# One transformer layer with a mixture of experts on one core: the last tile's router logits from its raw sum, and two pairs gathered by TensorE

## The chip, the core and the metric

The kernel runs on one core of one Trainium2 chip. What is compared is the device time of one execution, in microseconds (us). Engines are TensorE (PE in the profile; PEld is its weight load), VectorE (DVE), ScalarE (ACT), GpSimd (POOL) and SyncE (SP, which here only issues transfers; SPq is its queue).

## What is computed

One layer with a post-norm residual path, on 512 tokens of 1024 numbers:

```
h  <- LN(alpha*h + W_out[concat(norm(A(h)), norm(B(h)))])
h  <- LN(alpha*h + HierMoE(h))
...
gl = t @ w_group + b_group;  pg = softmax(gl);  g_idx = top_k(gl, 1)
el = (t @ w_expert + b_expert)[the 8 experts of g_idx]
top_v, top_i = top_k(el, 2);  w = pg[g_idx] * softmax(top_v)
for e in range(32):
    hid = silu(t @ w_gate[e]) * (t @ w_up[e])
    y   = y + combine[:, e:e+1] * (hid @ w_down[e])
```

A is an attention over a window of 128 positions to either side (8 heads of 64), B a dense latent attention (8 heads). Four groups of eight experts: a token goes to one group and in it to two experts.

## The kernel before

The 512 tokens are four tiles of 128 (0, 1, a = 2, b = 3). Attention B runs first, then attention A, tile after tile; then come for each tile the output projection of A's heads, the residual sum z, its layer norm, the router logits and the routing. For tiles 0 to 2 most of this lies between the matmuls of later tiles of attention A; for tile b it comes after the last attention matmul. Up to there a scheduler sets the order on each engine from the code's dependences, in the part of the experts the code's own order holds (`manual_schedule`).

The names of the routing, in the order of one tile: `turn` transposes the normed tile by TensorE, `logits` multiplies it with `wr` (the 4 columns of the groups and 32 of the experts), `biased` adds the bias (lgt), `route` finds the group and the two experts in ten short VectorE steps, and ends with Mb, a 0/1 matrix of token by expert; `count` and `place` make from it (by matmuls with triangular ones) the place of each token in its expert's 64 slots (posm); `weights` makes the two routing weights (cmb); `select` writes the 0/1 matrix of token by slot (sel); `places_mm` multiplies sel and cmb, so that each slot gets its token's number and weight, and `places_end` splits these.

The experts are handled in 16 pairs: a pair's 64 + 64 slots are the 128 rows of one tile. `fetch` lets POOL gather the tokens' rows from HBM by an indirect DMA (xg), `columns` transposes them (p_x to xT), `gates` runs the gate and up matmuls (p_gu, L1081, 8 steps k of 128 rows for two experts side by side), `gated` forms hid, `down` the second matmul (p_y, L1101), and `scatter` lets POOL write the weighted rows back to HBM (moe_rows) by an indirect DMA. The weights lie in a ring of 6 expert slots; `load_next` issues those of pair p + 3 on SyncE's queue behind the gates of pair p, in order. The last two pairs (14 and 15, `NCOMB`) are not scattered: their rows are combined on TensorE by products with sT (pz). In the end the two sets of 512 rows in HBM are loaded (rows0, rows1), summed, added to pz (`total`), normed (`square`, `factor`, `scale`, `gain`, `bias`) and written out.

The router's weights are loaded ahead of attention A, behind w_out's rows and the norm's factors:

```python
wr = rl_.tile([P, NK, 36], F32, name="wr")
SY.dma_start(out=wr[:, :, 0:4], in_=A["w_group"][0].rearrange("(k p) g -> p k g", p=P))
SY.dma_start(out=wr[:, :, 4:36], in_=A["w_expert"][0].rearrange("(k p) g -> p k g", p=P))
```

The `wout` generator loads w_out's rows and splits them into woah (ScalarE) and woal (VectorE, L521).

## Time and profile before

| | |
|---|---|
| time, median of 3 (lowest to highest) | 617.35 us (616.49 to 619.59) |
| profiled execution: time, span | 618.7 us, 617.0 us |
| mean granted clock of TensorE | 0.939 |
| busy: TensorE, VectorE, ScalarE, POOL | 534.0, 328.7, 204.7, 132.3 us |
| bytes over DMA | 137.91 MB, 223 GB/s over the span |

The busy times are sums over stages with different limits, so they say little alone; which engine or queue ends last is read by stretch. The clock is a share of full speed, and TensorE's two levels are 1.2 and 2.4 GHz, 0.5 and 1.0.

### The profile page before, as it was taken

What the parts mean: (1) busy time and instruction counts of PE and PEld (TensorE: products, weight loads), DVE (VectorE), ACT (ScalarE), POOL (GpSimd) and SP (SyncE); (2) the same over time, 40 slices, a digit from 0 to 9 for tenths busy, and PEclk for the clock granted to TensorE, in tenths of its full rate; (3) what the DMA queues carried; (4) which work ended last, traced back from release to release, by engine and by line L of the source; (5) the groups of instructions that cost most, each with busy time, mean ns of one, the idle gap of its engine ahead of it and who ended that gap; (6) DMA issues with size and microseconds to landing.
All of it is one profiled execution on the core that took longest, in us unless ns stands there. A gap on an engine that the chain in (4) does not pass through costs nothing. (4 is left out here: it accounts for less than half of the span.)

```text
span 617.0 us, 8276 instructions
## 1 busy us (share of the span) xinstructions
PE 534.0 (87%) x2886; PEld 341.7 (55%) x2887; DVE 328.7 (53%) x870; ACT 204.7 (33%) x428; POOL 132.3 (21%) x161
## 2 busy tenths in 40 slices
PE   3799999999899999999974899999997798768950
PEld 2688998799677777777763433333352232313330
DVE  5954465665896667977887343232431121102177
ACT  3174442544674356655510221112111010211131
POOL 2601122211433232213110211211111101000265
PEclk9799999999999999999985799999998899969975
DMA  8803400321220008960437499999999999998263
GB/s 293 246 2 78 136 1 18 107 79 39 86 70 1 1 1 242 396 258 36 172 114 295 122 381 421 416 412 420 419 412 409 420 412 385 422 420 330 76 257 136
DMA packets 42044, 137.91 MB, mean 223 GB/s; under 512 B 12168, under 2 KB 15112, under 8 KB 32784
## 3 DMA queue, kind: packets, MB, share of 16 engines
q1 hardware_dynamic: 36240, 126.86, 53.9%
q0 software_dynamic: 4608, 8.40, 3.7%
q10 hardware_dynamic: 1152, 2.10, 0.9%
q8 instruction: 24, 0.39, 0.3%
q14 instruction: 20, 0.16, 0.1%
HBM read 133.13 MB, written 12.58 MB: 236 GB/s over the span
## 5 line engine op out<-in xcount | busy, mean ns | idle before, releaser
L1081 PE MATMUL p_gu<-w_gu,xT 128*64 128x512 f32 x512 | 129.4, 626 | 16.9 <-DMA w_gu<-in_w_gu 16.9
L1081 PEld LDWEIGHTS p_gu<-w_gu,xT 128*64 128x64 f32 x512 | 41.5, 144 | 99.2 <-issue 73.3
L1086 DVE TENSOR_TENSOR hid<-hid,p_gu 128x256 f32<-128x256 f32 x16 | 6.7, 421 | 116.2 <-ACT hid L1085 116.2
L1101 PE MATMUL p_y<-w_dn,hidT 128*64 128x512 f32 x256 | 59.3, 598 | 1.1 <-issue 0.6
L1085 ACT ACTIVATE hid<-p_gu 128x256 f32<-128x256 f32 x16 | 6.1, 384 | 162.8 <-PE p_gu L1081 162.6
L1113 DVE SCALAR_TENSOR_TENSOR xg<-p_y,wsl,xg 128x512 f32<-128x512 f32 x28 | 21.0, 751 | 40.3 <-PE p_y L1101 40.0
L931 POOL DMA_INDIRECT xg<-norm_rows,tok x16 | 16.7, 1046 | 113.8 <-issue 39.0
L1106 POOL DMA_INDIRECT moe_rows<-xg,idx x16 | 16.5, 1033 | 109.7 <-DVE xg L1113 93.9
L1101 PEld LDWEIGHTS p_y<-w_dn,hidT 128*64 128x64 f32 x256 | 18.2, 137 | 30.8 <-issue 28.3
L592 PE MATMUL ptr<-cst,pr 128*128 128x128 f32 x208 | 34.7, 280 | 0.0
L554 POOL TENSOR_SCALAR pr<-pr,rc 128x512 f32<-128x512 f32 x16 | 25.0, 1565 | 43.6 <-DVE rc L553 43.6
L594 ACT COPY pT<-ptr 128x512 f32<-128x512 f32 (+2 forms) x48 | 22.6, 478 | 27.4 <-PE ptr L592 25.1
L592 PEld LDWEIGHTS ptr<-cst,pr 128*128 128x128 f32 x208 | 24.6, 141 | 7.5 <-issue 4.3
L567 ACT ACTIVATE pr<-pmm,bnm 128x512 f32<-128x512 f32 x32 | 22.1, 690 | 16.6 <-DVE bnm L564 13.8
L216 PE MATMUL pmm<-wh,htl 128*128 128x512 f32 (+1 forms) x64 | 24.1, 376 | 0.0
L214 PE MATMUL pmm<-wh,hth 128*128 128x512 f32 (+1 forms) x64 | 24.1, 376 | 0.0
L564 DVE TENSOR_REDUCE bnm<-pmm 128x1 f32<-128x512 f32 x32 | 21.8, 686 | 4.0 <-PE pmm L216 3.8
L215 PE MATMUL pmm<-wl,hth 128*128 128x512 f32 (+1 forms) x64 | 23.8, 372 | 0.0
L615 PE MATMUL pac<-pT,vb 128*64 128x128 f32 x256 | 23.7, 282 | 0.0
L1066 PEld LDWEIGHTS p_x<-cst,xg 128*128 128x128 f32 x128 | 14.8, 146 | 14.2 <-issue 8.1
L1066 PE MATMUL p_x<-cst,xg 128*128 128x128 f32 x128 | 20.6, 289 | 2.0 <-DMA xg<-norm_rows,tok 2.0
L586 ACT ACTIVATE pr<-sm,anm 128x257 f32<-128x257 f32 (+1 forms) x32 | 18.2, 569 | 12.2 <-PE ptr L592 6.1
(305 smaller groups left out, 1182.5 us busy)
## 6 DMA issues: line engine op xcount, KB each, us to landing
w_gu<-in_w_gu SPq DMA_DIRECT2D x52, 1024.0 KB, 16.5
...
```

The source lines that it names most:

```text
L214: PE.matmul(ps, ah, bh, start=first, stop=False)
L215: PE.matmul(ps, ah, bl, start=False, stop=False)
L216: PE.matmul(ps, al, bh, start=False, stop=last)
L554: eng.tensor_scalar(pr[:, :n], pr[:, :n], rc, None, ALU.mult)
L564: V.tensor_reduce(nm, sp, AX.X, ALU.max, negate=True)
L567: exps.append(SC.activation(pr[:, :S], sp, AF.Exp, bias=nm, accum_out=den).ins)
L592: PE.transpose(pt[:, k * P:(k + 1) * P], pr[:, k * P:(k + 1) * P], ident)
L594: ev(pT[:, :n * P], pt[:, :n * P])
L615: PE.matmul(po[64 * j:64 * j + 64, h0 // 2 * P:h0 // 2 * P + P], vfn(k0 + k, h), pp[j][:, k * P:(k + 1) * P], start=(k == 0), stop=(k == n ...
L1066: PE.transpose(pt[:, k], pl["xg"][:, P * (4 * j2 + k):P * (4 * j2 + k) + P], ident)
L1081: PE.matmul(pg[64 * i:64 * i + 64], xT[:, j, 64 * i:64 * i + 64], ws[i][0][j], start=(j == 0), stop=(j == 7))
L1101: PE.matmul(py[64 * i:64 * i + 64, :], hT[:, j, 64 * i:64 * i + 64], ws[i][1][n][:, j], start=(j == 0), stop=(j == 1))
```

## The change

Three things change. First, the last tile's logits no longer wait for its layer norm: ahead of attention A, wr is multiplied by the norm's gain and offset (wg, wb; gb_T is a new input that holds both, turned), and the column sums of both products are formed by 16 matmuls with ones. The last tile's raw sum is turned and multiplied with wg, and mean and deviation come in afterwards on the 36 logits. Second, the first two pairs are not fetched for their columns: TensorE multiplies the normed tiles with the 0/1 matrices sel0 (`gather`, 32 matmuls of 128x256), which gives xT directly; their rows are still fetched, for the residual. The first two pairs' weights come after the rows' numbers, and pair 0's gates are parted in steps 0 to 4 and 5 to 7 with the weights' matmuls between. Third, pair 14 is scattered as the others are, only pair 15 is combined by products, and the order at the end is written anew.

```diff
         lg2, lb2 = lngb[:, 0], lngb[:, 1]
+        gbT = rl_.tile([P, 2, NK], F32, name="gbT")
+        SY.dma_start(out=gbT, in_=A["gb_T"])
         wr = rl_.tile([P, NK, 36], F32, name="wr")
...
+        onesf = trif
+        V.memset(onesf, 1.0)
+        wg = rp_.tile([P, NK, 36], F32, name="wg")
+        wb = scr.tile([P, 385], F32, name="sm", bufs=2)[:, :NK * 36].rearrange("p (a b) -> p a b", a=NK)
+        for i, w_ in enumerate((wg, wb)):
+            V.tensor_tensor(w_, wr, gbT[:, i].unsqueeze(2).to_broadcast([P, NK, 36]), ALU.mult)
+        pgb = psd("sums")
+        for k in range(NK):
+            for i, w_ in enumerate((wg, wb)):
+                PE.matmul(pgb[:, 36 * i:36 * i + 36], onesf, w_[:, k], start=(k == 0 and i == 0), stop=(k == NK - 1 and i == 1))
+        wsum = rl_.tile([P, 36], F32, name="wsum")
+        SC.copy(wsum, pgb[:, 0:36])
+        rbias2 = rl_.tile([P, 36], F32, name="rbias2")
+        V.tensor_tensor(rbias2, pgb[:, 36:72], rbias, ALU.add)
+        sel0 = [rl_.tile([P, 4 * CAP], F32R, name="sel00")]
...
             for k in range(4 * i, 4 * i + 4):
-                PE.matmul(d["pl"][:, 0:36], d["hT"][i][:, k % 4 * P:k % 4 * P + P], wr[:, k, :], start=(k == 0), stop=(k == NK - 1))
+                w = wg[:, k, :] if t == NT - 1 else wr[:, k, :]
+                PE.matmul(d["pl"][:, 0:36], d["hT"][i][:, k % 4 * P:k % 4 * P + P], w, start=(k == 0), stop=(k == NK - 1))
         def biased(t):
             d = tl[t]
-            d["lgt"] = rl_.tile([P, 36], F32, name="lgt", bufs=2)
+            d["lgt"] = rl_.tile([P, 36], F32, name="lgt", bufs=3)
+            if t == NT - 1:
+                V.scalar_tensor_tensor(d["lgt"], wsum, d["nm"], d["pl"][:, 0:36], ALU.mult, ALU.add)
+                V.scalar_tensor_tensor(d["lgt"], d["lgt"], d["rs"], rbias2, ALU.mult, ALU.add)
+                return
             V.tensor_tensor(d["lgt"], d["pl"][:, 0:36], rbias, ALU.add)
...
+            if t == 1:
+                return
             yield
             for _ in route(t):
                 pass
             yield
+            rows_of(t)
             weights(t)
+            yield
+            count(t)
+            place(t)
+            sel0_(t)
...
+        def gather(t, js):
+            for j in js:
+                q = j // 2
+                if gk[q] is None:
+                    gk[q] = ps.tile([P, 2, 4, CAP], F32, name="p_g", tag="pmm" if q < 2 else "pwo", bufs=2)
+                PE.matmul(gk[q][:, j % 2].rearrange("p a b -> p (a b)"), z[t][:, P * j:P * j + P],
+                          f32v(sel0[t]),
+                          start=(t == 0 and j % 2 == 0), stop=(t == NT - 1 and j % 2 == 1))
...
-        for u in range(2):
-            count(u)
-            place(u)
+        offset(a)
+        r1 = route(1)
+        for _ in range(5):
+            next(r1)
         V.tensor_tensor(ol, pv, f32v(oh), ALU.subtract)
+        for i in range(2):
+            scaled(a, i)
+        gather(0, range(4))
         p0 = wout_h(0)
         V.tensor_reduce(s1, sq.rearrange("p a b -> p b a"), AX.X, ALU.add)
-        norm_gain(a, 0)
         sp = psd("sum")
...
+        for _ in r1:
+            pass
+        gain(a, 0, V)
         rsqrt(rr, sp[:, 0:1], ALPHA ** 2 / 512, ALPHA ** 2 * RMS_EPS)
+        gain(a, 1, V)
+        shift(a, 0, PO)
         wout_l(0, p0)
-        norm_bias(a, 0)
-        norm_gain(a, 1)
-        norm_bias(a, 1)
+        shift(a, 1, PO)
         wout_l(1, p1_)
+        norm_tiles(b)
+        turn(b, 0)
         turn(a, 1)
         for i in range(2):
             keep(a, i)
+        count(1)
+        place(1)
+        logits(a, 0)
...
+        V.tensor_scalar(nm, mv[:, 0:1], -1.0, None, ALU.mult)
         logits(a, 1)
-        norm_gain(b, 0)
-        norm_bias(b, 0)
-        norm_gain(b, 1)
-        turn(b, 0)
-        norm_bias(b, 1)
         turn(b, 1)
-        for i in range(2):
-            keep(b, i)
         biased(a)
         ra, rb = route(a), route(b)
         for _ in ra:
             pass
         logits(b, 0)
         logits(b, 1)
+        offset(b)
+        for i in range(2):
+            scaled(b, i)
+        biased(b)
         count(a)
-        biased(b)
+        gather(1, range(4))
         for _ in range(4):
             next(rb)
         place(a)
+        sel0_(a)
+        gain(b, 0, PO)
+        shift(b, 0, PO)
+        gather(0, range(4, 8))
         for _ in rb:
             pass
         count(b)
-        weights(a)
-        for t in range(b):
-            sel0_(t)
-        pi0 = psd("places")
-        cms0 = [weights_of(p) for p in range(2)]
-        places_mm(pi0, sel0, cms0, range(b))
+        gather(1, range(4, 8))
+        gather(a, range(8))
+        gain(b, 1, V)
         place(b)
         sel0_(b)
-        weights(b)
-        places_mm(pi0, sel0, cms0, [b])
-        pls = places_end(pi0, 2)
-        for p in range(2):
+        shift(b, 1, PO)
+        for i in range(2):
+            keep(b, i)
+        gather(b, range(8))
...
+        gathered(0)
+        gathered(1)
+        pi0 = psd("places")
+        pairs = range(2)
+        for t in range(NT):
+            for u in pairs:
+                PE.matmul(pi0[:, 2 * u:2 * u + 2], sel0[t][:, P * u:P * u + P],
+                          cmb[t][:, 2 * u:2 * u + 2, 0], start=(t == 0 and u == 0), stop=(t == b and u == 1))
+        pls = places_rows(pi0, 2, 2, 1)
+        for p in pairs:
             fetch(p, pls[p])
-        overflow()
+        for t in (1, a, b):
+            weights(t)
...
+        def run_pair(p, xT, nx, meanwhile):
             pg = new_gates()
-            gates(pg, xT, ws[p], 0, 8)
+            if p == 0:
+                gates(pg, xT, ws[p], 0, 5)
+                pi = psd("places")
+                places_mm(pi, sel0, [weights_of(u) for u in range(2)], range(NT))
+                places_weights(pi, pls, 6, 3, 1)
+                gates(pg, xT, ws[p], 5, 8)
+            else:
+                gates(pg, xT, ws[p], 0, 8)
             load_next(p)
...
+            def meanwhile(i):
+                if p == 0:
+                    if i == 0:
+                        group(1)
+                        for u in (2, 3):
+                            fetch(u, plc[u])
+                    else:
+                        for u in range(2):
+                            residual(u)
+                        overflow()
+                    return
...
+        p = NP - 2
+        pg = new_gates()
+        gates(pg, xTs[0], ws[p], 0, 8)
+        leave_rows(gated(pg), ws[p], plc[p])
         for t in range(NT):
             for k, r in enumerate((rows0, rows1)):
                 SY.dma_start(out=r[t], in_=yd[S * k + t * P:S * k + (t + 1) * P, :])
...
+        p = NP - 1
+        pg = new_gates()
+        gates(pg, xTs[1], ws[p], 0, 8)
+        hT = gated(pg)
+        y2 = [ring(slots(p)[0], f"gu0{k}", [P, D], F32R, "y2") for k in range(2)]
+        y2 = halves(y2)
+        weighted(p, hT, y2)
+        for t in range(NT):
+            for n in range(2):
+                pz_part(t, n, sTs[0], y2)
...
         gbs = gb[:, 0], gb[:, 1]
+        for t in range(2):
+            for n in range(2):
+                rows_add(t, n, PO)
+        for n in range(2):
+            rows_add(2, n, V)
         total(0)
-        rows_add(1, 1, PO)
-        rows_add(2, 0, PO)
+        square(0)
+        for n in range(2):
+            rows_add(3, n, V)
         total(1)
-        rows_add(2, 1, V)
-        square(0)
         factor(0, True)
+        scale(0)
         square(1)
-        scale(0)
+        total(2)
         factor(1, True)
-        total(2)
         square(2)
-        rows_add(3, 0, PO)
-        rows_add(3, 1, PO)
+        total(3)
+        gain(0)
+        square(3)
         scale(1)
-        gain(0)
-        total(3)
-        square(3)
         bias(0)
+        gain_first(2)
+        factor(2, False)
+        scale_bias(2)
         gain(1)
+        bias(1)
         factor(3, False)
-        factor(2, False)
         gain_first(3)
         scale_bias(3)
-        gain_first(2)
-        bias(1)
-        scale_bias(2)
```

Three places of VectorE's order, before and after. The first is the start of attention A (L580 before and L579 after are its scores, by a custom instruction; woal is w_out's lower part; wg and sm, which holds wb, are the two products).

Before:

```order
L564 TENSOR_REDUCE bnm<-pmm 128x1
L580 ISA sm,anm<-pmm,mask,nsink 128x256
L580 ISA anm 128x1
L553 RECIPROCAL rc<-den 128x1
L594 COPY pT<-ptr 128x512
L554 TENSOR_SCALAR pr<-pr,rc 128x512
L580 ISA sm,anm<-pmm,mask,nsink 128x256
L580 ISA anm 128x1
L553 RECIPROCAL rc<-den 128x1
```

After:

```order
L520 SCALAR_TENSOR_TENSOR woal<-wf_2586,goa,woah 128x1024
L547 SCALAR_TENSOR_TENSOR z_67<-pwo,rr,z_67 128x512
L520 SCALAR_TENSOR_TENSOR woal<-wf_2587,goa,woah 128x1024
L547 SCALAR_TENSOR_TENSOR z_67<-pwo,rr,z_67 128x512
L520 SCALAR_TENSOR_TENSOR woal<-wf_2587,goa,woah 128x1024
L709 TENSOR_TENSOR wg<-wr,gbT 128x288
L709 TENSOR_TENSOR sm<-wr,gbT 128x288
L579 ISA sm,anm<-pmm,mask,nsink 128x256
L579 ISA anm 128x1
L552 RECIPROCAL rc<-den 128x1
```

The products and all of woal stand ahead of the first scores; before, the first woal stood behind eight score instructions.

The second is where the last attention rows are split (aol) and squared sums taken (asum), at the end of attention A. Before:

```order
L832 TENSOR_TENSOR w_3560<-w_3560,e_3552 128x1
L834 TENSOR_SCALAR wc<-M_3519,w_3560 128x32
L719 SCALAR_TENSOR_TENSOR posm_78<-psd,Mb_69 128x32
L984 TENSOR_TENSOR aol<-pac,aoh 128x512
L986 TENSOR_REDUCE asum<-asq 128x128
L737 SCALAR_TENSOR_TENSOR z_66<-z_66,ln_mv,lngb 128x512
L835 SCALAR_TENSOR_TENSOR wc<-M_3555,w_3560,wc 128x32
```

After:

```order
L798 TENSOR_TENSOR lgt<-psd,rbias 128x36
L805 TENSOR_REDUCE gm<-lgt 128x1
L809 SCALAR_TENSOR_TENSOR fc<-lgt,gm,cst 128x4
L812 TENSOR_REDUCE fm<-fc 128x1
L815 TENSOR_SCALAR G<-fc,fm 128x4
L818 TENSOR_TENSOR em<-lgt,G 128x32
L1060 TENSOR_TENSOR aol<-pac,aoh 128x512
L1065 TENSOR_REDUCE asum<-asq 128x128
L823 MAX mm<-em 128x8
L826 MAX_INDEX mi<-mm,em 128x8
```

Before, tile 1's whole route and its place (posm_78) stood ahead of the split; now the first five steps of the route stand there, fed by logits that come later on TensorE, and the others stand behind.

The third is the second residual sum of tile b (the z_67 with pwo). Before:

```order
L976 SCALAR_TENSOR_TENSOR z_67<-pwo,rr,z_67 128x512
L998 BN_STATS ln_st<-z_67 128x6
L741 SCALAR_TENSOR_TENSOR z_66<-z_66,ln_rs,lngb 128x512
L976 SCALAR_TENSOR_TENSOR z_67<-pwo,rr,z_67 128x512
L1005 BN_STATS ln_st<-z_67 128x6
L1009 BN_AGGR ln_mv<-ln_st 128x2
```

After:

```order
L1024 SCALAR_TENSOR_TENSOR z_67<-pwo,rr,z_67 128x512
L1079 BN_STATS ln_st<-z_67 128x6
L1298 MEMSET silu 128x1
L737 SCALAR_TENSOR_TENSOR posm_78<-psd,Mb_69 128x32
L1024 SCALAR_TENSOR_TENSOR z_67<-pwo,rr,z_67 128x512
L1091 BN_STATS ln_st<-z_67 128x6
L922 TENSOR_TENSOR sel<-posm_78,cst 128x256
L1097 BN_AGGR ln_mv<-ln_st 128x2
```

The place of tile 1 (posm_78), which waits for a count on TensorE, now stands between the two sums.

## Rows read from the trace of the kernel before

**Rows 1.** Busy us by stretch (columns: PE, PEld, DVE, ACT, POOL, clock, DMA share, GB/s).

```profile
235.25:247.15 11.90, 11.80 (x91) 9.16 (x90) 10.72 (x40) 9.25 (x24) 1.52 (x7) 1.00 1.00 312
247.15:300.00 52.85, 51.91 (x353) 39.84 (x351) 43.90 (x141) 31.71 (x88) 12.07 (x31) 1.00 0.58 227
307.33:344.68 37.35, 21.66 (x112) 18.67 (x113) 29.72 (x127) 5.46 (x16) 5.58 (x6) 0.67 0.47 177
344.68:356.00 11.32, 10.94 (x53) 4.76 (x54) 2.40 (x5) 4.36 (x5) 0.86 (x1) 0.87 0.58 170
356.00:565.00 209.00, 185.80 (x858) 71.64 (x854) 57.77 (x154) 30.07 (x44) 26.79 (x26) 0.96 1.01 412
```

**Rows 2.** Timeline of VectorE at the start of attention A.

```profile
235.25 0.48 DVE L580 CUSTOM_DVE_ANT_0 sm<-pmm,mask,nsink 128x256 f32<-128x256 f32 x1 [0.93 <-PE pmm L577]
245.94 1.28 DVE L521 SCALAR_TENSOR_TENSOR woal<-wf,goa,woah 128x1024 fp32r<-128x1024 f32 x1
```

**Rows 3.** Timeline of SyncE's queue there: the issue of wr's second load.

```profile
236.67 4.34 SPq L693 DMA_DIRECT2D wr<-in_w_expert  x1
```

**Rows 4.** DMA view: packets from 242 to 244 us, and from 246 to 248 us.

```profile
DMA packets 1317, 0.64 MB, mean 321 GB/s; under 512 B 1170, under 2 KB 1170, under 8 KB 1317
DMA packets 194, 0.73 MB, mean 365 GB/s; under 512 B 19, under 2 KB 19, under 8 KB 191
```

**Rows 5.** Timeline of TensorE, end of attention to pair 0, and pair 15.

```profile
300.70 0.39 PE L215 MATMUL pwo<-woal,aoh 128*128 128x512 f32 x1
303.26 0.60 PE L758 MATMUL psd<-cst,z 128*128 128x128 f32 x4
304.87 1.87 PE L769 MATMUL psd<-wr,h2T 128*128 128x36 f32 x16
306.67 0.66 PE L615 MATMUL pac<-pT,va 128*64 128x128 f32 x8
323.61 3.43 PE L769 MATMUL psd<-wr,h2T 128*128 128x36 f32 x16
342.78 1.97 PE L1066 MATMUL p_x<-cst,xg 128*128 128x128 f32 x8 [1.96 <-DMA xg<-norm_rows,tok]
344.68 8.48 PE L1081 MATMUL p_gu<-w_gu,xT 128*64 128x512 f32 x32
576.11 3.65 PE L1081 MATMUL p_gu<-w_gu,xT 128*64 128x512 f32 x16
```

**Rows 6.** Timeline of VectorE from the end of attention to the first weights.

```profile
306.78 0.20 DVE L774 TENSOR_TENSOR lgt<-psd,rbias 128x36 f32<-128x36 f32 x1 [1.14 <-PE psd L769]
310.15 0.68 DVE L984 TENSOR_TENSOR aol<-pac,aoh 128x512 fp32r<-128x512 f32 x1
317.79 0.75 DVE L976 SCALAR_TENSOR_TENSOR z<-pwo,rr,z 128x512 f32<-128x512 f32 x1 [0.69 <-PE pwo L972]
329.62 0.15 DVE L816 TENSOR_SCALAR gn<-gm 128x1 f32<-128x1 f32 x1
331.56 0.20 DVE L837 TENSOR_TENSOR cmb<-wc,cmb 128x32 fp32r<-128x32 f32 x1
```

**Rows 7.** Timelines of ScalarE and of SyncE's queue at pair 0.

```profile
345.95 1.28 ACT L1085 ACT_TABLE_LOAD   x1
348.04 7.22 SPq L649 DMA_DIRECT2D w_gu<-in_w_gu  x6
```

**Rows 8.** Timelines of POOL, SyncE's queue and VectorE in the tail.

```profile
571.46 0.98 POOL L1106 DMA_INDIRECT moe_rows<-xg,idx  x1 [8.45 <-DMA moe_rows<-xg,idx]
581.05 1.80 POOL L1274 MEMSET gb<- 128x2048 f32 x1 [3.53 <-DMA moe_rows<-xg,idx]
599.23 2.94 POOL L1286 TENSOR_TENSOR rows<-rows,rows 128x512 f32<-128x512 f32 x2
584.36 4.47 SPq L1279 DMA_DIRECT2D rows<-moe_rows  x8
591.43 0.69 DVE L1326 CUSTOM_DVE_ANT_0 rows<-pz,rows 128x512 f32<-128x512 f32 x1 [0.49 <-POOL rows L1286]
```

184 lines of the change are left out of this document (95 added, 89 removed).

## The prediction

> **What bounds the kernel now.** I read the busy time by stretch first [rows 1]. From attention A's first scores (235.25) to 300 TensorE is busy nearly all the time: 11.80 of 11.90 us, then 51.91 of 52.85. Its last attention matmul ends at 307.33 [rows 5]; I call that point T0. From T0 to the first expert matmul at 344.68 TensorE is busy 21.66 of 37.35 us at a mean clock of 0.67 of full, and VectorE 29.72: there the chain of small routing steps decides. From 356 to 565 the DMA share is 1.01 at 412 GB/s: the weights of the experts stream in, and nothing else counts. The stream is kept going by the ring of weight slots, and it starts when the first expert pair's matmuls free a slot: SyncE issues w_gu at 348.04, and that group of six issues lasts 7.22 us, since its later tiles wait for the last matmuls of the pair [rows 7]. So each us by which pair 0's matmuls end later is a us at the end, and so is each us in the tail behind the stream; what a change costs between 356 and 565 on the engines is hidden by the DMA.
>
> **Term 1: the sums of the weighted router weights, ahead of attention A.** The change forms wg and wb on VectorE and sums them with 16 matmuls of 36 columns. In the new order of VectorE both products, and all four woal instructions, stand ahead of the first score instruction of attention A; before, eight score instructions stood ahead of the first woal. The products wait for wr. Its second load is issued from 236.67 and takes the queue 4.34 us [rows 3]; it consists of small packets: 1170 of 1317 packets in 242 to 244 are under 512 B, and 19 of 194 in 246 to 248 [rows 4]. So wr is there at about 246. The first score instruction, at 235.25 before [rows 2], then starts at about 247.5: 12.2 us later. Queued behind it are all scores, so the softmax, the transposes and the value matmuls of attention A. TensorE does not lose all of it. Part of its 11.80 us in this stretch was the end of attention B (a tile's output projection and the last value products), which it does in any case, and two units of scores fit into the two PSUM buffers ahead of VectorE. I put the lost work at 5.5 us, a little under half of the 11.80, and 1.5 for refilling the pipeline; neither is measured, so the ends stay far apart below. The 16 matmuls cost 16 x 0.234 = 3.7 us (eight of the same width took 1.87 us [rows 5]). Against it, tile 1's logits (1.87) and four of its transposes (0.6) move behind T0, and the four 1.28-us woal instructions [rows 2] no longer lie between scores, which I price at 1.5 to 2. Sum: 5.5 + 1.5 + 3.7 - 2.5 - 1.7 = +6.5 us on T0. Bounds: 0, if everything in this stretch can be caught up later (TensorE was busy 51.91 of 52.85 us after it, which speaks against that), and +12, if the whole shift passes on.
>
> **Term 2: from T0 to pair 0's first matmul.** Before, 37.35 us. Now TensorE's queue holds behind its last attention matmul: four gathers, four transposes of tile 1, eight output-projection matmuls, eight logits. A gather is a 128x256 f32 matmul; Eight of the experts' matmuls of 512 columns (16 records) took 3.65 us, and two of them run side by side, each on half of the array [rows 5]. On the whole array that is four matmuls of 512 columns or eight of 256: a gather is worth about 0.43 to 0.46 us. An output-projection matmul takes 0.233 (eleven from 300.70 to 303.26), four transposes 0.60, eight logits 1.87 [rows 5]. Queue: 4 x 0.43 + 0.6 + 8 x 0.233 + 1.9 = 6.1 us. VectorE takes tile 1's logits then, and the split aol of the attention rows stands behind five steps of this routing; before, routing had begun at 306.78, and aol ran at 310.15, T0 + 2.8 [rows 6]. Now aol is at 6.1 + 1.4 = T0 + 7.5 and the row sums end at about 9.1, 4.6 us later than before. Then the rest of the routing and a gain (2 us), the factor on POOL (1 us), two shifts on POOL at 1.47 each (two of its 128x512 sums took 2.94 [rows 8]), the transposes and the count that posm of tile 1 waits for; posm stands ahead of the second residual sum on VectorE, so that sum comes at about T0 + 17.5; before it ran at 317.79, T0 + 10.5 [rows 6]. Statistics and logits of the last tile follow; they are shorter than before, because the raw tile is turned and the row factors are applied to 36 logits: T0 + 22.5. Before, the last tile's logits ended at 327.04 at half clock [rows 5], T0 + 19.7. Now come 28 gathers, 28 x 0.43 = 12.0, which need nothing that is later than they are, and eight small matmuls for the rows (1.0): T0 + 35.9. What is gone: the wait of 1.96 us for the fetched rows and eight transposes of 1.97 us at the end of the chain [rows 5], the second tile's weights (329.62 to 331.76, 2.14 us [rows 6]), and the places behind them. Sum: 35.9 - 37.35 = -1.5 us. Bounds: -6 (the gathers fall into TensorE's idle 15.7 us, and what is gone, 1.96 + 1.97 + 2.14, is gained whole) and +4 (the gathers run at half clock for some of the time, as eight logits matmuls did in 3.43 us instead of 1.87).
>
> **Term 3: pair 0's matmuls.** They took 8.48 us, some of it at half clock [rows 5]; at full clock two times 3.65 less an overlap, 6.9. Now five of eight steps run, then TensorE waits for the weights of three tiles, which stand on VectorE behind the rows: 3 x 2.14 = 6.4 us from about T0 + 38, so to T0 + 44.4, while five steps end at 35.9 + 4.3 = 40.2. The stall is about 4.3 us; after it three steps take 2.6 us at full clock and 5.1 at half: the end is at T0 + 47.3 to 49.8, against T0 + 45.8 before (344.68 + 8.48 ends the block). So terms 2 and 3 together are +1.5 to +4.0; I take +2.75. Behind the stall SyncE waits with the later tiles of pair 3's w_gu, and the stream behind them. The four weight loads that moved there on the queue are done before the stream begins, and cost nothing as long as that holds. The exponentials in these weights come after the preload of Silu on ScalarE, so that the table is loaded back twice, 1.28 us each [rows 7]; one of them lies in the 6.4 us' way and is in the upper end.
> A rule of the Trainium skill bears on this: "ScalarE: Activation LUTs", What ACT_TABLE_LOAD costs, gives about 2.66 us for each switch of table sets, drain included. The row of 1.28 us shows the load alone, and ScalarE waits for TensorE behind it, so no run here shows the drain; by the page term 3 would be up to 1.4 us larger for each load on the path.
>
> **Term 4: the tail.** Pair 14 is no longer combined by products but scattered, so one more scatter must land before the rows are loaded; on the other hand TensorE has 16 product matmuls fewer. POOL's scatter waited from 563.0 to 571.46, the memset of gb begins at 581.05, and the loads of the rows are issued from 584.36 [rows 8]. With pair 14's scatter in the place of the second residual one, I get the loads at about 582.9, 1.5 us earlier. But on VectorE the sums of tile 2's rows now stand ahead of the first total, and wait for the sixth 512-KB load: the first total moves from 591.43 [rows 8] to about 597. Behind it are 8 totals (6.2), two sums (1.4), four gains and scalings in pairs of 1.4 to 2.4, and a wait for ScalarE's square of tile 1 behind scale 0 (2.2). I get an end about 3 us later; bounds -1.5 (the loads alone set the end) and +5.
>
> **Sum.** 6.5 + 2.75 + 3.0 = +12.25 us. The profiled execution took 618.7 (span 617.0), 1.35 above the median of 617.35; so I expect 631 for a profiled run and 629.5 for the median. About 0.5%, 3 us, is what a measurement of this kernel tells from no change.
>
> **Rivals.**
> A, faster, 611: wr's wait costs attention A nothing (the new order lets attention B's end run undisturbed, and TensorE makes up later), the gathers fit into idle time, pair 0's matmuls run as before, and the tail is even: 617.35 - 6.1. For it: the idle 15.7 us and the fetch at the end of the chain. Against it: 28 of the 32 gathers stand behind the last tile's logits, and the split of pair 0's matmuls waits for the weights. It decides where T0 moves by less than 1 us and the end of pair 0's matmuls comes before T0 + 43.
> B, no change, 617: terms 1 and 4 are small (+3, 0), and terms 2 and 3 give 3 back.
> C, worse, 636: the 12 us of VectorE's wait pass to T0 whole, plus terms 2 to 4: 617.35 + 12 + 2.75 + 3 = 635, or more with a half clock behind the stall.
>
> **Chances.** My forecast 0.55, A 0.20, B 0.10, C 0.15. Slower 0.70, same 0.10, faster 0.20. The likeliest's own range is 622 to 636; to hold 8 in 10 it must reach into A: 610 to 638.
>
> **What would show it.** Term 1: the first score instruction of attention A at 246 to 249, with TensorE idle for some us before it, and T0 at 310 to 317. Term 2: the last tile's logits at T0 + 22, then an unbroken block of gathers of 12 us. Term 3: TensorE idle inside pair 0's matmuls, and the DMA share as low as its 0.58 of 344.68 to 356 [rows 1] until about 362. Term 4: the first total behind tile 2's sum. I am wrong if VectorE's wait for wr is short (its load lands earlier), if T0 does not move, or if the share of DMA reaches 1 before 356.

## The result

The changed kernel took 640.25 us (median of 4 runs, 639.29 to 640.97) against 617.76 us: ratio 1.0361, 95% interval 1.033 to 1.0391. It is slower by some 22.5 us. Slower was forecast, but the time lies above the range of 610 to 638; the term for attention A was a little over half of what came (6.5 of 11.7 us), and the tail cost more than its term, at another place. The profiled execution has a span of 638.3 us, 21.3 more than before, and a mean clock of 0.938.

Five points in time place the difference. T0 is the end of the last attention matmul; "issue" is SyncE's issue of the row loads in the tail; "end" is the end of VectorE's last instruction.

| | T0 | pair 0's gates begin | end | row loads' issue | VectorE's end |
|---|---|---|---|---|---|
| before | 307.33 | 344.68 | 353.16 | 584.36 | 613.65 |
| after | 319.01 | 356.13 | 368.88 | 600.08 | 634.96 |
| longer by, in each stretch | +11.7 | -0.2 | +4.3 | 0.0 | +5.6 |

From the end of pair 0's gates to the row loads both take 231.2 us. The stretches sum to 21.3.

The busy time by stretch of the kernel after, with the columns of [rows 1]:

```profile
235.25:247.15 11.90, 10.10 (x65) 7.28 (x63) 7.68 (x13) 5.92 (x7) 1.67 (x2) 1.00 0.99 325
251.70:265.50 13.80, 13.80 (x60) 11.01 (x59) 6.40 (x27) 6.32 (x21) 1.47 (x8) 0.51 1.02 419
319.01:356.13 37.12, 33.35 (x177) 28.84 (x176) 21.39 (x73) 10.04 (x19) 8.04 (x7) 0.86 0.46 170
356.13:370.00 13.87, 11.36 (x50) 4.75 (x50) 6.74 (x42) 4.46 (x13) 2.29 (x2) 0.88 0.32 101
370.00:584.00 214.00, 188.09 (x868) 71.98 (x867) 62.75 (x176) 31.43 (x45) 28.83 (x28) 0.95 1.01 408
```

The stretch of 11.9 us in which TensorE was busy 11.80 now has 10.10. Then comes one that had no counterpart: from 251.70 to 265.50 TensorE is busy without a gap and its mean clock is 0.51: of the two levels, 1.2 and 2.4 GHz, it is at the lower. The routing stretch, 37.12 us, has TensorE busy 33.35 instead of 21.66: the gathers fill it and it is no shorter. Behind it, from 356.13 to 370, the DMA share is 0.32 where it was 0.58; from 370 the stream runs as before.

VectorE at the start of attention A (timeline; compare [rows 2]):

```profile
247.83 1.27 DVE L520 SCALAR_TENSOR_TENSOR woal<-wf,goa,woah 128x1024 fp32r<-128x1024 f32 x1
249.02 0.45 DVE L709 TENSOR_TENSOR wg<-wr,gbT 128x288 f32<-128x288 f32 x1
249.39 0.45 DVE L709 TENSOR_TENSOR sm<-wr,gbT 128x288 f32<-128x288 f32 x1
249.75 0.48 DVE L579 CUSTOM_DVE_ANT_0 sm<-pmm,mask,nsink 128x256 f32<-128x256 f32 x1
```

The first score instruction runs at 249.75, 14.5 us later than at 235.25. No row of the two products has an idle time ahead of it: VectorE does not wait for wr, it is busy with woal and with attention B's last sums, which stand ahead in its queue.

TensorE (timeline; compare [rows 5]):

```profile
249.52 0.41 PE L713 MATMUL psd<-wg,trif 128*128 128x36 f32 x2 [2.74 <-DVE wg L709]
252.02 0.62 PE L713 MATMUL psd<-wg,trif 128*128 128x36 f32 x2
...
318.36 0.65 PE L614 MATMUL pac<-pT,va 128*64 128x128 f32 x6
318.94 1.99 PE L1034 MATMUL p_g<-sel,z 128*128 128x256 f32 x8
346.53 8.88 PE L1034 MATMUL p_g<-sel,z 128*128 128x256 f32 x40
356.13 4.51 PE L1183 MATMUL p_gu<-w_gu,xT 128*64 128x512 f32 x20
361.96 0.39 PE L941 MATMUL psd<-cmb,sel 128*128 128x6 f32 x2 [0.78 <-DVE gn L847]
364.08 0.39 PE L941 MATMUL psd<-cmb,sel 128*128 128x6 f32 x2 [1.74 <-DVE cmb L864]
364.39 4.49 PE L1183 MATMUL p_gu<-w_gu,xT 128*64 128x512 f32 x12
```

It stands idle for 2.74 us, then runs the 16 narrow sums, of which a record of two takes 0.39 us at first and 0.62 from 252.02 on. Behind T0 come eight records of gathers, and later 56; 40 of them in one piece from 346.53. In pair 0's gates lies the wait for the weights, 0.78 and 1.74 us and the matmuls between.

VectorE at the boundary and in the tail, and SyncE's queue (timelines; compare [rows 6 to 8]):

VectorE:

```profile
324.99 0.20 DVE L798 TENSOR_TENSOR lgt<-psd,rbias 128x36 f32<-128x36 f32 x1 [5.98 <-PE psd L788]
326.24 0.68 DVE L1060 TENSOR_TENSOR aol<-pac,aoh 128x512 fp32r<-128x512 f32 x1
336.28 0.74 DVE L1024 SCALAR_TENSOR_TENSOR z<-pwo,rr,z 128x512 f32<-128x512 f32 x1
...
601.84 0.40 DVE L1188 TENSOR_TENSOR hid<-hid,p_gu 128x256 f32<-128x256 f32 x1
612.35 0.68 DVE L1441 CUSTOM_DVE_ANT_0 rows<-pz,rows 128x512 f32<-128x512 f32 x1
```

SyncE's queue:

```profile
358.09 12.80 SPq L648 DMA_DIRECT2D w_gu<-in_w_gu  x6
...
600.08 4.37 SPq L1420 DMA_DIRECT2D rows<-moe_rows  x8
```

Tile 1's logits come at T0 + 6.0, the split right behind at 326.24, T0 + 7.2, and the second residual sum at T0 + 17.3. The issue of pair 3's w_gu begins 2 us into pair 0's gates and takes 12.80 us instead of 7.22. In the tail pair 15's hid runs at 601.84, though ScalarE had its part at 595.60, since the shuffles of gb stand ahead on VectorE.

### The profile page after: what moved, and what is told of

It reads as the page before. It is cut to its first block, busy times and chain, and to the rows that moved or that the text cites. A ratio compares the mean times of both kernels' runs of the same rounds, so it can differ in the third digit from the quotient of the medians.

```text
span 638.3 us, 8415 instructions
## 1 busy us (share of the span) xinstructions
PE 552.9 (87%) x2954; PEld 356.2 (56%) x2955; DVE 332.0 (52%) x878; ACT 208.6 (33%) x435; POOL 134.8 (21%) x164
## 5 line engine op out<-in xcount | busy, mean ns | idle before, releaser
L1183 PE MATMUL p_gu<-w_gu,xT 128*64 128x512 f32 x512 | 128.1, 626 | 16.6 <-DMA w_gu<-in_w_gu 16.6
L1203 PE MATMUL p_y<-w_dn,hidT 128*64 128x512 f32 x256 | 63.8, 636 | 2.1 <-DVE pm L872 0.6
L1215 DVE SCALAR_TENSOR_TENSOR xg<-p_y,wsl,xg 128x512 f32<-128x512 f32 x30 | 22.5, 751 | 42.6 <-PE p_y L1203 42.1
L591 PE MATMUL ptr<-cst,pr 128*128 128x128 f32 x208 | 36.0, 288 | 0.0
L553 DVE TENSOR_SCALAR pr<-pr,rc 128x512 f32<-128x512 f32 (+2 forms) x48 | 21.0, 441 | 1.0
L215 PE MATMUL pwo<-wh,htl 128*128 128x512 f32 (+1 forms) x56 | 20.8, 371 | 0.0
```

The source lines that it names most:

```text
L215: PE.matmul(ps, al, bh, start=False, stop=last)
L553: eng.tensor_scalar(pr[:, :n], pr[:, :n], rc, None, ALU.mult)
L591: PE.transpose(pt[:, k * P:(k + 1) * P], pr[:, k * P:(k + 1) * P], ident)
L1183: PE.matmul(pg[64 * i:64 * i + 64], xT[:, j, 64 * i:64 * i + 64], ws[i][0][j], start=(j == 0), stop=(j == 7))
L1203: PE.matmul(py[64 * i:64 * i + 64, :], hT[:, j, 64 * i:64 * i + 64], ws[i][1][n][:, j], start=(j == 0), stop=(j == 1))
L1215: V.scalar_tensor_tensor(y, py, pl["wsl"], y, ALU.mult, ALU.add)
```

## Experiments

Times are medians; the kernel before took 617.8 to 618.9 beside them. The table at the end of this section has the stretches of each.

**Sums alone, on the kernel before.** Two runs add the products and the 16 matmuls to the kernel before and use nothing of them; the turned tile has three buffers in place of four, for space. They differ in where wb lies: in a score buffer (first line), or in a buffer of the turned tile (second).

```diff
+        wb = scr.tile([P, 385], F32, name="sm", bufs=2)[:, :NK * 36]...
+        wb = rp_.tile([P, 512], F32, name="h2T", bufs=3)[:, :NK * 36]...
```

> The kernel before, with only the router sums added (products wg and wb, 16 matmuls), wb in one of the two score buffers as in the change; the results are not used, and the turned tile has three buffers in place of four. Theory (the buffer puts the products and woal ahead of the first scores, attention A starts late and then runs at half clock): first scores at about 249, the last attention matmul 12 to 14 us later than 307.33, time 629 to 632. Rival (the sums cost only their matmuls, 16 x 0.234 = 3.7 us): 621 to 622.

Measured: 633.63 us, ratio 1.024 (1.0216 to 1.0263), 1.6 above its interval; first score at 250.90, T0 at 322.17. This part of the change by itself gives two thirds of its loss. Here the clock is at 0.50 before the first of the sums begins, inside TensorE's wait for the products (windows, then TensorE's timeline):

```profile
250.25:250.50 0.25, 0.00 (x0) 0.00 (x0) 0.25 (x1) 0.00 (x0) 0.00 (x0) 0.50 1.34 492
```

```profile
250.67 0.64 PE L713 MATMUL psd<-wg,trif 128*128 128x36 f32 x2 [2.74 <-DVE wg L709]
```

> The same addition to the kernel before, but wb in a buffer of the turned tile instead of a score buffer. Theory (the shared buffer is the cause): first scores at 235, the last attention matmul 3 to 4.5 us later than 307.33, time 620 to 622. Rival (the wait for wr and the extra work are the cause, wherever wb lies): as the run beside it, 629 to 632.

Measured: 625.60 us, 1.0093 (1.0056 to 1.0129), 3.6 above its interval; first score at 234.44, T0 at 315.11. The order of the two kernels differs as the theory says: with wb in a score buffer the products stand ahead of the first score, otherwise eight scores stand ahead of them. But T0 is 7.8 us later than 307.33, and not 3 to 4.5: behind the sums TensorE ran at half clock for 6.8 us (2-us windows), which is 3.4 us of work; with the matmuls, 3.74, and 0.5 us more idle time that makes 7.6.

**The changed kernel with wb elsewhere.**

```diff
-        wb = scr.tile([P, 385], F32, name="sm", bufs=2)[:, :NK * 36]...
+        wb = rp_.tile([P, 512], F32, name="h2T", bufs=3)[:, :NK * 36]...
```

> The changed kernel with one edit: wb in a buffer of the turned tile instead of a score buffer. Theory: first scores back at 235, the last attention matmul at 308 to 310 instead of 319.0, time 629 to 631 against 640. Rival (late start comes from wr's load or from the order of woal itself): no change, 639 to 641.

Measured: 633.56 us, 1.0207 (1.0166 to 1.0248), 2.6 above its interval. The first score is back at 235.52, T0 at 313.55: 5.5 us of the 11.7 came from the buffer. Of these, 1.9 are idle time of TensorE (240 to T0: 1.44 us instead of 3.31) and 3.4 a half clock of 6.8 us instead of 13.7. 309 was expected; what is left is seen in the windows of this run from 255 to 265:

```profile
255.00:260.00 5.00, 4.22 (x34) 3.81 (x33) 4.70 (x14) 3.13 (x8) 0.37 (x2) 0.89 1.02 421
260.00:265.00 5.00, 5.00 (x20) 4.60 (x21) 1.02 (x4) 1.16 (x4) 0.18 (x1) 0.50 1.02 419
```

TensorE has the same 0.78 us of idle time in this stretch as the kernel before, whose clock stays at 1.00, and the clock is at 0.50 from 260 on. The block of narrow matmuls began at 256.75 and the records grew from 0.39 to 0.62 us inside it.

**Idle time filled.** 14 matmuls without use, ahead of the sums:

```diff
+        for _ in range(14):
+            PE.matmul(pgb, woah[0][:, 0:P], woah[1][:, 0:512], start=True, stop=True)
```

> The changed kernel with 14 matmuls without use (128x512, one pass, about 0.23 us each) on TensorE ahead of the sums, so that it does not stand idle from 246.8 to 249.5; the start of the scores stays as late as it is. Theory (a good half of the 11.7 us is the half clock from 251.7 to 265): the clock stays at full, the last attention matmul 5 to 7 us earlier than 319.0, time 633 to 635. Rival (the late start alone): time 640, or 0.5 us more for the matmuls added.

Measured: 636.58 us, 1.0295 (1.0265 to 1.0324); T0 at 317.39. The time lies between the theory and the rival: the wait for the products shrank from 2.74 to 1.2 us, the products came at 251.31, later than 249.02, and the clock still fell among the sums, for 6.8 us. So the theory that filling the wait keeps the clock failed; as 1.2 us of the wait were left, this run alone doesn't tell the wait from the sums.

**Sums with half as many matmuls.** wg and wb side by side, so that a matmul has 72 columns:

```diff
-                PE.matmul(pgb[:, 36 * i:36 * i + 36], onesf, w_[:, k], ...)
+                PE.matmul(pgb[:, 0:72], onesf, wq[:, k], ...)
```

> The run with wb outside the score buffers, with the router sums in 8 matmuls of 72 columns instead of 16 of 36. Theory (the clock falls to half inside the block of 16 narrow matmuls, with no idle time, and stays there for 7 us): with half as many it does not fall, the last attention matmul at about 308.5 instead of 313.9, time 628 to 629.5 against 633.6. Rival (the clock falls from the wait of 0.78 us ahead of them, which the kernel before has too): only 1.9 us less work, 631.5 to 632.5.

Measured: 625.07 us, 1.0121 (1.009 to 1.0152), 2.9 below its interval: 8.5 us less than with wb elsewhere alone. T0 is 306.45, 0.9 us ahead of the kernel before. The windows from 255 to 265, and the two blocks of sums on TensorE's timeline:

```profile
255.00:260.00 5.00, 4.72 (x35) 4.29 (x36) 4.17 (x16) 3.04 (x9) 0.59 (x2) 1.00 1.02 419
260.00:265.00 5.00, 5.00 (x35) 3.77 (x33) 2.99 (x10) 2.32 (x7) 0.70 (x3) 1.00 1.02 424
```

```profile
255.86 1.11 PE L715 MATMUL psd<-h2T,trif 128*128 128x72 f32 x8
257.32 1.00 PE L715 MATMUL psd<-h2T,trif 128*128 128x72 f32 x8
```

The clock stays at 1.00, and the eight matmuls (four in each row) take 1.11 and 1.00 us, less than the 3.74 that 16 cost at full clock. The last test keeps all of this kernel and parts each matmul in two of 36 columns again:

```diff
+                for i in range(2):
+                    PE.matmul(pgb[:, 36 * i:36 * i + 36], onesf, wq[:, k, 36 * i:36 * i + 36], ...)
```

> As the run with 8 matmuls of 72 columns, but each as two of 36: 16 narrow matmuls, 9 and 5 of them in a row with two projection matmuls between, and two later. Theory (a long row of narrow matmuls is what takes the clock down): the clock falls between 258 and 266, time 629 to 633 against 625.1. Rival (where the buffers lie and the order of the rest made the difference, not the matmuls): 625 to 627, the clock stays.

Measured: 632.52 us, 1.0208 (1.0175 to 1.0241); T0 at 314.09. The clock fell again (windows):

```profile
255.00:260.00 5.00, 4.22 (x33) 3.72 (x33) 4.96 (x18) 3.13 (x8) 0.59 (x2) 0.96 1.02 423
260.00:265.00 5.00, 5.00 (x23) 4.91 (x22) 1.53 (x4) 0.19 (x1) 0.00 (x0) 0.50 1.02 421
```

So with wb outside the score buffers it is the long row of narrow matmuls that decides whether the clock falls: both kernels have the idle time of 0.78 us (with 72 columns it begins ahead of 255), and so has the kernel before. T0 differs by 7.6 us between these two. Of these, 3.4 are the half clock (6.8 us of it), 1.6 the matmuls themselves at full clock and 0.3 idle time; 1.5 lie ahead of the sums (attention B's last product ends at 240.11 with 72 columns, at 241.57 here), and some 0.8 us I can't place.

With wb in a score buffer the wait of 2.74 us stands ahead of the row as well. There the clock fell 1.0 to 2.3 us into the row in four of the seven kernels, and inside the wait, before the first of the sums, in the other three (the first run above, and below the gates in one block and the shuffles with the old order). So in the changed kernel the row and the wait can each take the clock down. Wide sums with wb in a score buffer, which would keep the wait and take the row away, were not run.

**The boundary: the split first.** On the changed kernel:

```diff
-        for _ in range(5):
-            next(r1)
         V.tensor_tensor(ol, pv, f32v(oh), ALU.subtract)
...
         rsqrt(rr, sp[:, 0:1], ALPHA ** 2 / 512, ALPHA ** 2 * RMS_EPS)
+        for _ in range(5):
+            next(r1)
...
+        add_z(1, p1_)
         count(1)
         place(1)
-        add_z(1, p1_)
```

> The changed kernel with VectorE's order behind the last attention matmul changed: the split of the attention rows, their squared sums and the factor stand ahead of tile 1's routing, and tile 1's place behind the second residual sum. Theory (the split waits for tile 1's logits): the split at T0 + 1.5 instead of T0 + 7.2, the first gate matmul at T0 + 32 to 34 instead of T0 + 37.1, time 635 to 637. Rival (the 28 gathers wait for tile a's norm and routing, which come no earlier): 639 to 641.

Measured: 637.51 us, 1.0319 (1.029 to 1.0349). The split ran at 320.47, T0 + 1.2, the second residual sum at T0 + 12.6 instead of T0 + 17.3, and the first gate matmul at T0 + 34.5 instead of 37.1. Of 4.7 us at the sum 2.6 reach the gates, 0.5 less than the least expected, and the time lies 0.5 above its interval. The stall in pair 0 got shorter too, so that the gates end at T0 + 45.6 instead of 49.9.

**Pair 0's gates in one block.**

```diff
-                gates(pg, xT, ws[p], 0, 5)
+                gates(pg, xT, ws[p], 0, 8)
                 pi = psd("places")
                 places_mm(pi, sel0, [weights_of(u) for u in range(2)], range(NT))
                 places_weights(pi, pls, 6, 3, 1)
-                gates(pg, xT, ws[p], 5, 8)
```

> The changed kernel with one edit: pair 0's eight gate steps in one block, the weights' matmuls behind them. Theory (the stall inside the block holds back the later tiles of pair 3's loads and so the whole stream): the block takes 7 to 8.5 us instead of 12.75, the stream and the end come 4 to 5 us earlier, 635 to 636 against 640.25. Rival (the stream waits for something else at that place): 639 to 641.

Measured: 636.25 us, 1.0281 (1.0248 to 1.0314), 0.25 above its interval. TensorE and SyncE's queue (timelines):

TensorE:

```profile
360.46 7.09 PE L1183 MATMUL p_gu<-w_gu,xT 128*64 128x512 f32 x32
367.48 1.33 PE L941 MATMUL psd<-cmb,sel 128*128 128x6 f32 x8
```

SyncE's queue:

```profile
362.43 7.18 SPq L648 DMA_DIRECT2D w_gu<-in_w_gu  x6
```

The block takes 7.09 us instead of 12.75, the issue of pair 3's w_gu 7.18 instead of 12.80, and the time falls by 4.0. The gates end at T0 + 45.2 instead of 49.9; from there to the row loads it is 232.7 us instead of 231.2, so that some of the gain is lost again behind them. The weights' matmuls now stand between the gates and pair 0's second matmul, which begins at T0 + 50.2 instead of 53.2: of 4.7 us 3.1 reach it.

**The tail.** Three edits on the changed kernel. First, tile 2's row sums behind two totals:

```diff
-        for n in range(2):
-            rows_add(2, n, V)
         total(0)
         square(0)
-        for n in range(2):
-            rows_add(3, n, V)
         total(1)
+        for n in range(2):
+            rows_add(2, n, V)
+        for n in range(2):
+            rows_add(3, n, V)
```

> The changed kernel with one edit in the tail: VectorE's sums of tile 2's rows stand behind the totals of tiles 0 and 1 instead of ahead of the first total. Theory (the first total waits there for tile 2's rows): the first total at about 609.7 instead of 612.35, time 1.5 to 2.5 us less, 638 to 638.7. Rival (the end is set by ScalarE's and POOL's chain behind the squares): 640 within 0.7.

Measured: 639.32 us, 1.0322 (1.0277 to 1.0366), no difference that can be told from 640.25, as the rival had it. From the issue of the row loads to VectorE's end it took 35.6 us, after 34.9. The first total ran at 612.43, 11.5 us behind the issue, on VectorE right behind pair 15's second y, which began at 611.76 when ScalarE's part came: pair 15's hid had been late, at 602.94, behind the shuffles of gb. So the next edit puts these shuffles behind the hid:

```diff
-        for i in range(2):
-            for n in range(2):
-                V.stream_shuffle(gb[:, i, ...], gb[:, i, ...], [0] * 32)
         p = NP - 1
         pg = new_gates()
         gates(pg, xTs[1], ws[p], 0, 8)
         hT = gated(pg)
+        for i in range(2):
+            for n in range(2):
+                V.stream_shuffle(gb[:, i, ...], gb[:, i, ...], [0] * 32)
```

> The changed kernel with one edit in the tail: the four shuffles of gb stand on VectorE behind pair 15's hid and hidT instead of ahead of them. Theory (pair 15's hid waits 6 us behind the shuffles, which wait for gb's load, and everything behind it with it): hid at 596 instead of 601.84, TensorE's wait of 6.73 us gone, the second matmuls of pair 15 at full clock, the end 3 to 5 us earlier, 635.5 to 637.5 against 640.25. Rival (the end is set by the loads of the rows, issued at 600.08): 639 to 641.

Measured: 641.06 us, 1.0374 (1.0344 to 1.0404), no gain. VectorE's timeline:

```profile
597.34 0.42 DVE L1188 TENSOR_TENSOR hid<-hid,p_gu 128x256 f32<-128x256 f32 x1 [6.53 <-ACT hid L1187]
611.91 1.29 DVE L1412 TENSOR_TENSOR rows<-rows,rows 128x512 f32<-128x512 f32 x2 [7.97 <-DMA rows<-moe_rows]
613.13 0.68 DVE L1441 CUSTOM_DVE_ANT_0 rows<-pz,rows 128x512 f32<-128x512 f32 x1
```

hid runs at 597.34, 0.4 us behind ScalarE's part, and pair 15's products are done by 607.3; but the first total now waits at 611.91 for tile 2's rows and runs at 613.13, 12.9 us behind the issue. Each wait covered the other here; what both together are worth is seen below. The third run has the shuffles so and the old order of the end (POOL takes six row sums, VectorE two; tile 0's factor ahead of tile 2's total):

```diff
-        for t in range(2):
-            for n in range(2):
-                rows_add(t, n, PO)
-        for n in range(2):
-            rows_add(2, n, V)
+        rows_add(0, 1, V)
+        rows_add(0, 0, PO)
+        rows_add(1, 0, PO)
         total(0)
...
+        rows_add(1, 1, PO)
+        rows_add(2, 0, PO)
         total(1)
+        rows_add(2, 1, V)
...
```

> The changed kernel with the shuffles behind pair 15's hid and the order of the kernel before in the tail, nothing else. Theory: the tail gives back 4 to 5.6 us, 634.5 to 636.5 against 640 to 641. Rival (the loads of the rows set the end): 639.5 to 641.

Measured: 636.56 us, 1.026 (1.0219 to 1.0301). From 602.64 (issue) to 631.57 (end) it took 28.9 us: 6.0 less, and as in the kernel before (29.3).

**All together.** The sums in 8 matmuls, the split first, the gates in one block and the shuffles moved; then the same with tile 2's sums moved, then with the old order of the end.

> Four edits of the runs so far together: the sums in 8 matmuls outside the score buffers, the split ahead of tile 1's routing, pair 0's gates in one block, the shuffles behind pair 15's hid. Theory (each cost is on the path and they add up; from 625.1 with the first alone, 2 to 3 less for the split, 3 to 4 for the gates, 3 to 5 for the shuffles): 613 to 617, at or below the kernel before at 618. Rival (the stream of weights has a start of its own behind pair 0, and takes back what the boundary gives): 619 to 622.

> The same with VectorE's sums of tile 2's rows behind the totals of tiles 0 and 1 too. Theory: with pair 15's products early, the first total now does wait for tile 2's rows, and the edit that gave nothing alone gives 1 to 2.5 us: 611 to 616. Rival: no difference from the run beside it.

> The four edits together, and in the tail the order of the kernel before from the first row sum on (POOL takes six of eight row sums, tile 0's factor comes ahead of tile 2's total), with pair 15 alone by products. Theory (the 5.6 us that the tail takes longer from the issue of the row loads to the end, 34.9 against 29.3, are the new order: two row sums more on VectorE, tile 0's factor late, tile 1's square behind tile 0's scaling): issue to VectorE's end 29 to 30.5 us, time 612 to 614.5. Rival (the tail is longer since the rows of pair 14 come as loads and not as products): 33 us or more, 617 to 618.

Measured: 618.61 us, ratio 1.0013 (0.9997 to 1.003); 617.22, 0.9988 (0.9971 to 1.0004); and 612.72, 0.9908 (0.9886 to 0.993). The first two miss their intervals by 1 to 2 us, and the last lies in its interval and is 0.9% faster than the kernel before. The second takes both waits of the tail away: its first total runs 6.7 us behind the issue, against 11.5 in the first. Yet from issue to end it takes 33.8 us, against 34.2, and by the medians it is 1.4 us faster. So the two waits are worth little of the 5 us that the old order gives. What sets the end is the order behind the first total, which comes 7.2 us behind the issue in the third kernel, no earlier than in the second. VectorE in the second kernel and then in the third, at tile 0's factor (timelines; the row loads are issued at 579.79 and 579.07):

```profile
593.84 1.29 DVE L1413 TENSOR_TENSOR rows<-rows,rows 128x512 f32<-128x512 f32 x2 [0.28 <-DMA rows<-moe_rows]
595.05 0.15 DVE L181 TENSOR_SCALAR rsq_t<-st 128x1 f32<-128x1 f32 x1
```

```profile
590.77 0.92 DVE L1413 TENSOR_TENSOR rows<-rows,rows 128x512 f32<-128x512 f32 x1
591.61 0.14 DVE L181 TENSOR_SCALAR rsq_t<-st 128x1 f32<-128x1 f32 x1
```

In the second kernel the factor stands behind the sums of tile 3, which wait for the last of the eight loads, and runs 15.3 us behind the issue; in the third, 12.5. Tile 1's factor runs 19.0 us behind it, and in the third 13.1. The scaling of four tiles comes behind it. Tile 0's factor is 2.8 of the 5.0 us between the two; the rest (the second's wait of 2.18 us for ScalarE's square, and the division of the last products between POOL and VectorE) was not parted. The third kernel's row loads on SyncE's queue and VectorE's last group:

```profile
579.07 3.87 SPq L1421 DMA_DIRECT2D rows<-moe_rows  x8
```

```profile
606.42 1.40 DVE L1473 SCALAR_TENSOR_TENSOR rows<-rows,st,gb 128x512 f32<-128x512 f32 x2
```

| | T0 | gates begin, end (from T0) | gates' end to issue | issue to end | time |
|---|---|---|---|---|---|
| before | 307.33 | 37.4, 45.8 | 231.2 | 29.3 | 617.8 |
| after | 319.01 | 37.1, 49.9 | 231.2 | 34.9 | 640.25 |
| sums alone, score buffer | 322.17 | 37.0, 45.9 | 230.3 | 28.6 | 633.63 |
| sums alone, other buffer | 315.11 | 38.6, 47.2 | 230.8 | 28.8 | 625.60 |
| wb elsewhere | 313.55 | 37.7, 51.4 | 230.3 | 34.8 | 633.56 |
| filled | 317.39 | 37.2, 48.2 | 230.3 | 34.3 | 636.58 |
| 8 of 72 columns | 306.45 | 37.1, 48.2 | 230.2 | 34.7 | 625.07 |
| 16 of 36 again | 314.09 | 37.8, 51.6 | 229.9 | 35.0 | 632.52 |
| split first | 319.31 | 34.5, 45.6 | 230.2 | 35.2 | 637.51 |
| gates whole | 322.34 | 38.1, 45.2 | 232.7 | 34.7 | 636.25 |
| tile 2's sums later | 321.16 | 37.1, 49.6 | 230.2 | 35.6 | 639.32 |
| shuffles later | 320.26 | 37.4, 50.2 | 229.8 | 35.5 | 641.06 |
| shuffles, old order | 322.86 | 37.1, 49.6 | 230.2 | 28.9 | 636.56 |
| four edits | 306.79 | 33.4, 40.5 | 231.1 | 34.2 | 618.61 |
| four, tile 2's sums | 307.08 | 33.4, 40.4 | 232.3 | 33.8 | 617.22 |
| four, old order | 307.01 | 33.4, 40.4 | 231.6 | 28.8 | 612.72 |

The columns are from the profiled executions, the times are medians. T0 lies between 319.0 and 322.9 in the six kernels whose code up to there is that of the changed one: the half clock at the sums lasts 13.6 to 20.5 us in them (2-us windows), the longest where T0 is latest, so that small differences of their times say little, and the columns counted from T0 say more. Some of the spread of T0 lies ahead of the sums: attention B's last product ends between 238.95 and 241.57 in the 16 kernels. From there to T0 it is 66.6 us before, 66.3 in the four kernels with sums of 72 columns, 72.5 in the two with wb elsewhere and 36 columns, and 79.8 to 82.4 in these six.

## Why the prediction was wrong

**What bounds the kernel** held. From the end of pair 0's gates to the row loads it is 229.8 to 232.7 us in all 16 kernels, whatever came ahead: a shift ahead of it passes to the end, but for these 2.9 us.

**Term 1, +6.5 us, was +11.7.** TensorE from 240 to T0, before and after (busy time by stretch):

```profile
240.00:307.33 67.33, 66.30 (x457) 1.00 0.61 224
```

```profile
240.00:319.01 79.01, 75.70 (x466) 0.91 0.51 186
```

Idle time grew from 1.03 to 3.31 us, +2.3. The clock's mean of 0.91 is the 13.8 us at half clock, 6.9 us of work. The remaining 2.5 are work: the 16 matmuls, less what left the stretch, and less 1.5 us by which the changed kernel was ahead at 240 (attention B's last product ends at 239.25 instead of 240.73; counted from there the term is +13.2). The first score was late as predicted, by a little more (14.5 us instead of 12.2), but not because of wr's load: VectorE stood in its own queue behind woal and attention B's sums. For lost work and refill 7.0 us had been set, a little under half of 11.80 and 1.5; idle time says 2.3, since TensorE had the end of attention B and the sums to do. The step that failed outright is "the 16 matmuls cost 16 x 0.234 = 3.7 us". That is their price at full clock, from a row in which only eight such matmuls stood together [rows 5], and a fall of the clock there was put at nothing. In the changed kernel the clock fell to 0.50 in the middle of the 16, 2.3 us behind the end of TensorE's wait, and stayed there over attention's work. With wb elsewhere the row of 16 did this without that wait; in three kernels the wait did it ahead of the row; which of the two it was in this execution stays open. With half as many, wider sums, the clock kept and the buffer free, the whole term is -0.9 us on T0, and -0.3 counted from attention B's last product. Rival C's price, 12 us on T0, was met, but half of it by a mechanism that no rival had.

The Trainium skill, "TensorE: Matmul & The Clock Gate", What's actually happening, has the lower clock as the state of an engine that has been idle, which activity releases. Where the clock fell inside the wait of 2.74 us, the rows are in line with that. With wb elsewhere they are not: the idle time ahead was the 0.78 us that the kernel before has too, and TensorE counts as busy for 5.00 of 5.00 us from 260 to 265, at 0.50. There the measurement decides.

**Term 2, -1.5, was -0.2**, inside its bounds. (Its own steps, 22.5 + 12.0 + 1.0, end at T0 + 35.5 and not 35.9, so that they give -1.9; and term 3's, 44.4 + 2.6 and 44.4 + 5.1, end 0.3 us ahead of the 47.3 and 49.8 written. Neither decides anything.) The split at T0 + 7.2 (7.5 predicted), the second residual sum at T0 + 17.3 (17.5) and the block of gathers came as worked out; some of the gathers ran at a lower clock, at 0.86 over the stretch. Of the 4.7 us by which the second residual sum can come earlier, 2.6 reach the gates.

**Terms 2 and 3 together, +2.75 with an upper end of +4.0, were +4.0.** Pair 0's gates took 12.75 us: the three steps behind the stall took 4.49 us at a mean clock of 0.62, most of it at half clock, near to the 5.1 of the upper end. Pulling them together gave 4.7 us from T0 on and 4.0 us of time. That upper end also had a table load in it, and it was not on the path. ScalarE (timeline):

```profile
355.53 1.28 ACT L850 ACT_TABLE_LOAD   x1
357.74 0.30 ACT L850 ACTIVATE ge<-lgt,gn 128x4 f32<-128x4 f32 x1 [0.93 <-DVE gn L847]
362.56 1.28 ACT L1187 ACT_TABLE_LOAD   x1
368.96 0.38 ACT L1187 ACTIVATE hid<-p_gu 128x256 f32<-128x256 f32 x1 [5.12 <-PE p_gu L1183]
```

The first load ends 0.9 us before gn is there, the second 5.1 us before the gates' products are. By the Trainium skill, "ScalarE: Activation LUTs", What ACT_TABLE_LOAD costs, each load on the path would have cost up to 1.4 us more. Neither was on it. With the gates in one block the second load is on it, and shows what it costs there (ScalarE, timeline):

```profile
366.91 1.28 ACT L1187 ACT_TABLE_LOAD   x1
368.20 0.39 ACT L1187 ACTIVATE hid<-p_gu 128x256 f32<-128x256 f32 x1
```

ScalarE's instruction ahead of the load ends at 366.90, the gates at 367.55, and hid starts at 368.20, right behind the load. The switch takes 1.30 us there with nothing of the 1.4 us beside it, and the measurement decides. The prediction says that no run shows this; in the kernel before, too, a load at 38.31 is followed by the next instruction at 39.60.

**Term 4, +3.0 with an end of +5, was +5.6, at another place.** The row loads came no earlier against pair 0's end (0.0 instead of -1.5). The step that failed is "the first total moves from 591.43 to about 597", as the cause of the later end: the wait for tile 2's rows, and the wait for pair 15's hid that lay over it, can both be taken away and 33.8 of 34.9 us stay. The first total did move, from 7.1 us behind the issue to 12.3; it is not what the end waits for. The order behind the first total is what costs: with the old order the stretch is 28.8 to 28.9 us, and between the two runs with only the shuffles moved it is an edit of the order alone that takes it from 35.5 to 28.9. Shown is that sum, and the factor's place in it; the other parts stay open.

**The sum.** In the profiled execution the half clock is 6.9 us of work. By an estimate from this figure the changed kernel without it would lie at about 633.4 us, inside the range, and 3.9 above the value named. The time is 2.25 us above the range, and the 2.6 us by which the tail exceeded its term would have been enough too, so the miss of the range rests on both, and for the larger part on the clock. That the kernel is slower rests on the order and on the places that the prediction named. Some of it is luck: in term 1 the lost work, 7.0 us set and 2.3 measured, was too high by 4.7 and hid that much of the clock's 6.9.

## What to carry to other kernels

A tile borrowed from a ring of buffers borrows its place in the order as well: the next user waits for the borrower's last reader, and a scheduler then puts everything the borrower needs ahead of it. Look for such an alias in the order before the price of the work itself. Price a block of many narrow matmuls not only by their sum: read the granted clock behind such a block, and prefer fewer, wider ones. And where a chain's first step can be made earlier and the end stays, read the order of the steps behind it; undo waits together before calling a place free.

## What the runs showed that had not been expected

TensorE's clock fell from 2.4 to 1.2 GHz in the three kernels with wb elsewhere and sums of 36 columns, without idle time ahead of it that the kernel before did not have. It fell 2.1 to 2.3 us into a row of 16 matmuls of 128x36 (or of 9 and 5 with two others between), and it stayed up with 4 and 4 matmuls of 128x72 at the same place: 0.50 against 1.00 from 260 to 265. With a wait of 2.74 us ahead of the row it fell inside the row or already inside the wait, and stayed low for longer: it came back after 6.8 us in the four runs with wb elsewhere or with filled idle time, and after 13.6 to 20.5 in the seven others with wb in a score buffer, nearly all of it work that keeps TensorE busy.

VectorE's scalings are slower beside POOL's products in the tail. POOL and then VectorE in the kernel with the four edits and tile 2's sums moved (timelines):

```profile
601.14 3.31 POOL L1478 TENSOR_TENSOR rows<-rows,gb 128x512 f32<-128x512 f32 x2 [1.25 <-DVE rows L1463]
605.14 0.55 POOL L183 TENSOR_TENSOR st<-rsq_t,mhalf 128x1 f32<-128x1 f32 x1 [0.69 <-DVE rsq_t L181]
607.82 3.31 POOL L1478 TENSOR_TENSOR rows<-rows,gb 128x512 f32<-128x512 f32 x2 [2.13 <-DVE rows L1463]
```

```profile
601.58 3.42 DVE L1468 SCALAR_TENSOR_TENSOR rows<-rows,st,gb 128x512 f32<-128x512 f32 x2
605.73 1.41 DVE L1473 SCALAR_TENSOR_TENSOR rows<-rows,st,gb 128x512 f32<-128x512 f32 x2 [0.66 <-POOL st L183]
```

Two scalings of 128x512 take VectorE 3.42 us beside POOL's two products, and 1.41 while POOL stands still. What this costs POOL, these rows don't show.
